# A hybrid decoder trunk on one core: scaling on GpSimd, evictions after the next split, and a new order of the first loads

## The chip, the cores and the metric

The kernel runs on one core of one Trainium2 chip. The metric is the device time of one execution in microseconds; the median of three runs is taken. A core has TensorE (matmuls; PE in the profile), VectorE (DVE), ScalarE (ACT), GpSimd (POOL) and SyncE (SP, here only a queue that issues DMAs). Each engine works through its own queue in order.

## The reference, cut to what matters

One layer on 256 rows of 2048 float32 values: a norm, one wide projection, attention with three branches beside a gated convolution, an output projection, and a gated MLP with a short convolution.

```
h     = rms_norm(x, mix_norm_g)
q, kv, gate_logits, conv_in = split(h @ w_in)
gates = sigmoid(gate_logits)
attn  = gates[0]*o_cmp + gates[1]*o_sel + gates[2]*o_win    # three softmax attentions, 16 heads
conv  = silu(layer_norm(causal_conv_31(a * sigmoid(g))))    # a, g = halves of conv_in
x     = x + concat(attn, conv) @ w_out
h     = rms_norm(x, ffn_norm_g)
x     = x + (silu(gate) * a) @ w_down                       # a, gate = causal_conv_3(h @ w_up)
out   = rms_norm(x, final_norm_g)
```

## The kernel before

Every float32 matrix product is made of three matmuls on a high and a low part (`mm3`, `mm_rows`). So each weight chunk (128 x 2048 float32, 1 MB) is loaded to `wraw` (`w_dma`, on SP's queue), split by ScalarE into the high part `wh` (L109) and by VectorE or GpSimd into the low part `wl` (L114), and then used by TensorE. Three buffers of each kind stand behind this, and the split runs two chunks ahead (`LA`). For chunks `POOLED[0] <= c < POOLED[1]` the low part is GpSimd's. `w_split` puts a chunk's split into `pieces`; `w_pump` emits them, some at each `hook`, of which each chunk has four.

The chunks in order: 0 and 1 come with the columns of x in the block `head`, loaded and split in the pieces that `CUTS` names; 2 to 15 are the convolution's gate and value tiles (`gb`, `ab`, two per j); 16 to 19 the keys and values of the compressed branch; 20 to 23 the keys; 24 to 29 the values and gates (`v_evac`); 30 to 37 the queries; then the output projection, w_up and w_down. The norm of x is not applied to x: TensorE works on x, and the evictions multiply by the inverse norm, which `x_rstd` makes from the rows of x (`xr`), `x_diag` and `x_spread` spread into `rB`.

The order in each queue is the order in which the program emits the work. An eviction is emitted after its chunk's last matmul, ahead of the next chunk's `w_next`. Lists of small steps are emitted at the hooks: `steps`, and `side`, the 30 taps of the long convolution on VectorE (L363), whose pace a planner's clock sets (`fill`). `tab_neg` (L283) and, seven hooks later, `tab_rel` (a matmul, L287) make the table of position biases.

During the q chunks from the second on, `attn_tick` advances the attention of 32 units by one stage: scores, minimum with bias (L632), exponential with its sum (L643), reciprocal (L651), scaling by reciprocal and gate (`st_scale`, L658), transposes (L664), their eviction `es` (L669) and the products (L677). The scaling of a unit is one tick ahead of its transposes. Between them run the splits, the q evictions, and the convolution's norm (`ck` is one of its small copies).

The functions that the diff touches, and their callers:

Of the kernel before, what the change touches and what calls it, by code (L numbers as in the profile page):

```python
# [18 lines left out]
T = 256  # L19
# [16 lines left out]
POOLED = (3, 30)  # L36

CUTS = ((0, 2), (2, 4), (4, 8), (8, 12), (12, 16))
# [8 lines left out]
def hybrid_trunk(ctx: ExitStack, tc: tile.TileContext, a: dict, out: bass.AP):  # L47
# [32 lines left out]
    raws, parts, pieces = {}, {}, []  # L80
    clock = {"pe": 0.0, "dve": 0.0}
# [43 lines left out]
    def w_next(cuts=1, ahead=LA):  # L125
        c = st["use"]
        st["use"] += 1
        w_pump()
        while st["split"] <= min(c + ahead, len(chunks) - 1):
            w_pump()  # L130
            w_split(cuts)
        if cuts == 1:
            w_pump()
        return parts.pop(c)
# [54 lines left out]
    with ExitStack() as mx:  # L189
# [9 lines left out]
        def load_small():  # L199
            nc.scalar.dma_start(oh, a["onehot"])  # L200
            nc.scalar.dma_start(rbn[:32], a["rel_slots"])
            nc.scalar.dma_start(cw, a["conv_vecs"])
# [7 lines left out]
        for n, (lo, hi) in enumerate(CUTS):  # L210
            w = 512 * (hi - lo)
            tile_, c0 = (ha, at) if n < 3 else (hb4[n - 3], 0)
# [4 lines left out]
        w_dma()  # L217
# [3 lines left out]
        w_dma()  # L221
        w_dma()
# [162 lines left out]
        for j in range(8):  # L385
            gb, ab = [b[:, :T] for b in bank[2 * (j if j < 3 else (j + 1) % 2):][:2]]
            if j == 0:
# [6 lines left out]
                w_pump()  # L394
                x_rstd()
# [4 lines left out]
                load_small()  # L400
                first = gb, ab
                continue
            tile_chunk(gb)
            if j == 1:
                steps[:0] = [x_diag, lambda: None, x_spread]
                tile_chunk(ab)
                glu(0, first[1], glu_gate(first[0]))
                glu(1, ab, glu_gate(gb))
            else:
                sg = glu_gate(gb)  # L410
                tile_chunk(ab)
                glu(j, ab, sg)
# [70 lines left out]
        for n in range(4):  # L483
            tile_chunk(bank[n][:, :T])
# [4 lines left out]
            for r in range(2):  # L489
# [4 lines left out]
                nc.scalar.activation(k_l[o, r, q, br], k_l[h, r, q, br].bitcast(F32), AF.Copy)  # L494

# [24 lines left out]
        for t in range(2):  # L520
            v_evac(t, 0, vb[t][:, :256])
# [13 lines left out]
        for t in range(2):  # L535
            v_evac(t, 1, vb[t][:, :256])
            gsrc = vb[t][:, 256:304].rearrange("p (q r g b) -> p b q g r", q=2, r=2, g=4)
            for br in range(3):
                nc.scalar.activation(gates[:, br, :, t].rearrange("p (q g r) -> p q g r", q=2, r=2),
                                     gsrc[:, br], AF.Sigmoid, scale=rc[:, t:t + 1])  # L540

        nc.vector.tensor_scalar(alive, wb[:, 0, CU0:CU0 + 1], BIG / 2, None, op0=OP.is_lt)
# [549 lines left out]
```

## Time and profile before

| | before |
|---|---|
| median of 3 runs | 1164.25 us (1162.98 to 1164.31) |
| the profiled execution, its own time | 1164.46 us |
| its span, first to last instruction | 1162.7 us |
| mean granted TensorE clock | 0.993 |
| TensorE busy | 1136.0 us |
| VectorE, ScalarE, GpSimd busy | 748.7, 582.3, 128.2 us |

Times in the rows are in us from the span's start unless marked ns. A granted clock of 1.00 is full speed. A wait is put down to the instruction that ended it. The prediction takes its terms from one execution and sums them against that execution's own time.

### The profile page before, as it was taken

How to read it: one execution, taken by the hardware profiler on the slowest of the kernel's cores; microseconds unless marked ns; L12 is line 12 of the kernel's file. 1: busy time of each engine (PE TensorE's matmuls, PEld its weight loads, DVE VectorE, ACT ScalarE, POOL GpSimd, SP SyncE). 2: the span in 40 equal slices, each digit the busy share in tenths (PEclk: the TensorE clock that was granted, in tenths of full speed). 3: DMA queues.
4: the chain of work that ended last, by engine and by line, in shares of the span. 5: the costliest groups of instructions: out<-in, count | busy, mean ns of one | idle time of the engine just before them, and what ended most of it. 6: DMA issues, size and time to landing. Idle time of an engine off the chain costs nothing.

```text
span 1162.7 us, 18834 instructions
## 1 busy us (share of the span) xinstructions
PE 1136.0 (98%) x7890; PEld 1058.0 (91%) x7890; DVE 748.7 (64%) x1162; ACT 582.3 (50%) x810; POOL 128.2 (11%) x80
## 2 busy tenths in 40 slices
PE   8999999889899999999999999999999999999997
PEld 8999999888778899999999999999999888888886
DVE  6699569676455666667666666666666655556544
ACT  6534256788754544444535444544454444444443
POOL 1979553000000000000000000000000000000000
PEclk9999999999999999999999999999999999999998
DMA  9567416222264545545554545454545555555551
GB/s 367 194 240 260 152 53 252 73 79 94 70 265 152 211 169 194 204 160 183 181 215 147 198 174 209 145 215 171 196 149 210 191 182 203 185 185 181 182 180 73
DMA packets 32290, 207.62 MB, mean 179 GB/s; under 512 B 3867, under 2 KB 6187, under 8 KB 8012
## 3 DMA queue, kind: packets, MB, share of 16 engines
q1 hardware_dynamic: 28592, 199.64, 48.0%
q10 hardware_dynamic: 3612, 6.76, 1.6%
q8 instruction: 62, 1.02, 0.4%
q14 instruction: 24, 0.20, 0.1%
HBM read 204.27 MB, written 2.12 MB: 178 GB/s over the span
## 4 chain that ended last, share of the span: by engine, by line
PE 87%; ACT 5%; DVE 4%; DMA 2%; issue 1%; POOL 1%; DVEq 0%; POOLq 0%; ACTq 0%
PE bank L139 18%; PE bank L137 18%; PE bank L138 18%; PE bank L146 9%; PE bank L145 9%; PE bank L144 9%; DMA xr<-in_x 2%; ACT wh L109 1%; PE bank L437 1%; ACT e L643 1%; DVE wl L114 1%; PE bank L677 1%; ACT e L658 1%; PE bank L664 1%; POOL wl L114 0%
## 5 line engine op out<-in xcount | busy, mean ns | idle before, releaser
L137 PE MATMUL bank<-xt_h,wh 128*128 128x256 f32 x1920 | 546.9, 285 | 1.8 <-ACT wh L238 1.7
L139 PE MATMUL bank<-xt_h,wl 128*128 128x256 f32 x1920 | 544.8, 284 | 1.8 <-POOL wl L114 1.5
L138 PE MATMUL bank<-xt_l,wh 128*128 128x256 f32 x1920 | 544.5, 284 | 0.0
L114 DVE TENSOR_TENSOR wl<-wraw,wh 128x2048 fp32r<-128x2048 f32 (+1 forms) x185 | 360.6, 1967 | 126.9 <-ACT wh L109 126.8
L109 ACT ACTIVATE wh<-wraw 128x2048 fp32r<-128x2048 f32 (+2 forms) x239 | 352.7, 1501 | 135.7 <-PE bank L146 68.7
L137 PEld LDWEIGHTS bank<-xt_h,wh 128*128 128x128 f32 x1920 | 369.3, 192 | 3.9 <-ACT wh L238 2.5
L139 PEld LDWEIGHTS bank<-xt_h,wl 128*128 128x128 f32 x1920 | 369.3, 192 | 2.4 <-POOL wl L114 1.7
L138 PEld LDWEIGHTS bank<-xt_l,wh 128*128 128x128 f32 x1920 | 369.5, 192 | 0.7
L900 ACT ACTIVATE yt<-u,vecs 128x256 f32<-128x256 f32 x88 | 53.0, 603 | 204.0 <-DVE u L898 204.0
L144 PE MATMUL bank<-wh,gh 128*128 128x512 f32 (+1 forms) x360 | 140.8, 391 | 0.0
L146 PE MATMUL bank<-wh,gl 128*128 128x512 f32 (+1 forms) x360 | 140.8, 391 | 0.0
L145 PE MATMUL bank<-wl,gh 128*128 128x512 f32 (+1 forms) x360 | 140.8, 391 | 0.0
L903 DVE SCALAR_TENSOR_TENSOR yt<-u,vecs,yt 128x255 f32<-128x255 f32 (+1 forms) x176 | 85.1, 484 | 62.2 <-ACT yt L900 59.1
L114 POOL TENSOR_TENSOR wl<-wraw,wh 128x1024 fp32r<-128x1024 f32 (+1 forms) x54 | 120.7, 2271 | 36.1 <-ACT wh L109 36.1
L173 POOL TENSOR_TENSOR rstd<-ms,half 128x1 f32<-128x1 f32 x4 | 2.2, 549 | 876.0 <-DVE ms L166 876.0
L363 DVE SCALAR_TENSOR_TENSOR bank<-us,cw,bank 128x256 f32<-128x256 f32 x232 | 93.7, 483 | 4.2 <-ACT bank L358 3.7
L146 PEld LDWEIGHTS bank<-wh,gl 128*128 128x128 f32 x360 | 67.8, 188 | 15.8
L145 PEld LDWEIGHTS bank<-wl,gh 128*128 128x128 f32 x360 | 67.8, 188 | 15.8
L144 PEld LDWEIGHTS bank<-wh,gh 128*128 128x128 f32 x360 | 67.8, 188 | 15.8
L892 ACT ACTIVATE gh<-gt 128x1024 fp32r<-128x1024 f32 x22 | 23.3, 1059 | 64.6 <-PE bank L145 64.6
L898 DVE TENSOR_TENSOR u<-bank,rB 128x256 f32<-128x256 f32 x88 | 37.0, 420 | 26.3 <-PE bank L139 26.3
L893 DVE TENSOR_TENSOR gl<-gt,gh 128x1024 fp32r<-128x1024 f32 x22 | 27.0, 1225 | 41.0 <-ACT gh L892 41.0
(179 smaller groups left out, 860.4 us busy)
## 6 DMA issues: line engine op xcount, KB each, us to landing
wraw<-in_w_u SPq DMA_DIRECT2D x88, 1024.0 KB, 5.0
wraw<-in_w_d SPq DMA_DIRECT2D x44, 1024.0 KB, 4.9
wraw<-in_w_t SPq DMA_DIRECT2D x30, 1024.0 KB, 4.8
wraw<-in_w_o SPq DMA_DIRECT2D x16, 1024.0 KB, 4.9
wraw<-in_w_vg SPq DMA_DIRECT2D x4, 608.0 KB, 3.7
hb<-in_head SPq DMA_DIRECT2D x2, 1024.0 KB, 10.8
xr<-in_x SPq DMA_DIRECT2D x2, 1024.0 KB, 16.9
wb<-rel_scratch ACTq DMA_DIRECT2D x1, 2048.0 KB, 10.8
```

The lines of the kernel that those rows point to most:

```text
L109: nc.scalar.activation(h[:, sl], raw[:, sl], AF.Copy)
L114: (nc.gpsimd if pooled else nc.vector).tensor_sub(l[:, sl], raw[:, sl], h[:, sl].bitcast(F32))
L137: nc.tensor.matmul(ps, wh, xh, start=first, stop=False)
L138: nc.tensor.matmul(ps, wh, xl, start=False, stop=False)
L139: nc.tensor.matmul(ps, wl, xh, start=False, stop=last)
L144: nc.tensor.matmul(ps, xh, wh, start=first, stop=False)
L145: nc.tensor.matmul(ps, xh, wl, start=False, stop=False)
L146: nc.tensor.matmul(ps, xl, wh, start=False, stop=last)
L363: nc.vector.scalar_tensor_tensor(y[:, j] if last else acc[0], us[:, j, k:k + T], cw[:, j, k:k + 1], acc[0], op0=OP.mult, op1=OP.add)
L898: nc.vector.tensor_mul(u, bank[:, :T], rB)
L900: nc.scalar.activation(yt, u, AF.Identity, scale=fcw[:, c, 2:3], bias=fcw[:, c, 3:4])
L903: nc.vector.scalar_tensor_tensor(yt[:, d:], u[:, :T - d], fcw[:, c, k:k + 1], yt[:, d:], op0=OP.mult, op1=OP.add)
```

## The change

In words, part by part:

- `st_scale`: the two multiplications of a unit go from ScalarE to GpSimd.
- `POOLED` is (5, 32) in place of (3, 30): chunks 3 and 4 get their low part from VectorE, chunks 30 and 31 from GpSimd.
- A list `late`: evictions are put on it, and `w_next` of the next chunk emits them after that chunk's call of the split; for a pooled chunk the whole split is emitted first. This holds for the convolution's gates and values from j = 2 on, the keys, the values and gates, and the queries.
- `CUTS` has six pieces in place of five: k-tiles 4 to 8 come in two loads of 512 KB.
- The loads of chunks 2, 3 and 4 are issued in front of the rows of x; before, only chunk 2 was. The three small loads go from ScalarE's queue to SP's, behind x.
- `x_rstd` and two memsets move behind the first tile of j = 1, and the spread and the first two convolution tiles' evictions become steps of the chunk after j = 1.

```diff
-POOLED = (3, 30)
-
-CUTS = ((0, 2), (2, 4), (4, 8), (8, 12), (12, 16))
+POOLED = (5, 32)
+
+CUTS = ((0, 2), (2, 4), (4, 6), (6, 8), (8, 12), (12, 16))
...
+    late = []
...
         while st["split"] <= min(c + ahead, len(chunks) - 1):
             w_pump()
             w_split(cuts)
-        if cuts == 1:
+        if cuts == 1 or POOLED[0] <= st["split"] - 1 < POOLED[1]:
             w_pump()
+        now = late[:]
+        late.clear()
+        for f in now:
+            f()
         return parts.pop(c)
...
         def load_small():
-            nc.scalar.dma_start(oh, a["onehot"])
-            nc.scalar.dma_start(rbn[:32], a["rel_slots"])
-            nc.scalar.dma_start(cw, a["conv_vecs"])
+            nc.sync.dma_start(oh, a["onehot"])
+            nc.sync.dma_start(rbn[:32], a["rel_slots"])
+            nc.sync.dma_start(cw, a["conv_vecs"])
...
-            tile_, c0 = (ha, at) if n < 3 else (hb4[n - 3], 0)
+            tile_, c0 = (ha, at) if n < 4 else (hb4[n - 4], 0)
...
-        w_dma()
+        for _ in range(3):
+            w_dma()
         xr = [ap.tile([P, D], F32, name=f"xr{t}", tag=tg) for t, tg in enumerate(("y", "us"))]
         for t in range(2):
             nc.sync.dma_start(xr[t], x_rows[:, t])
-        w_dma()
-        w_dma()
+        load_small()
...
                 w_pump()
+                first = gb, ab
+                continue
+            tile_chunk(gb)
+            if j == 1:
                 x_rstd()
                 tok = ap.tile([P, 2, 5, P], F32, name="tok", tag="tok")
                 nc.gpsimd.memset(tok[:, :, 4], 0.0)
                 us = ap.tile([P, 8, PADT], F32, name="us", tag="us")
                 nc.gpsimd.memset(us[:, :, :TAPS - 1], 0.0)
-                load_small()
-                first = gb, ab
-                continue
-            tile_chunk(gb)
-            if j == 1:
-                steps[:0] = [x_diag, lambda: None, x_spread]
                 tile_chunk(ab)
-                glu(0, first[1], glu_gate(first[0]))
-                glu(1, ab, glu_gate(gb))
+                steps[:0] = [x_diag, x_spread, lambda: glu(0, first[1], glu_gate(first[0])),
+                             lambda gb=gb, ab=ab: glu(1, ab, glu_gate(gb))]
             else:
-                sg = glu_gate(gb)
+                sg = []
+                late.append(lambda gb=gb, sg=sg: sg.append(glu_gate(gb)))
                 tile_chunk(ab)
-                glu(j, ab, sg)
+                late.append(lambda j=j, ab=ab, sg=sg: glu(j, ab, sg[0]))
...
+        for n in range(4):
+            tile_chunk(bank[n][:, :T])
+            late.append(lambda n=n: k_evac(n))
...
-        for t in range(2):
-            v_evac(t, 0, vb[t][:, :256])
+        late.extend(lambda t=t, src=vb[t][:, :256]: v_evac(t, 0, src) for t in range(2))
...
+        late.append(vg_evac)
...
-                nc.scalar.activation(e[:, lo:hi], e[:, lo:hi], AF.Copy, scale=lsum[:, br, t:t + 1])
+                nc.gpsimd.tensor_scalar_mul(e[:, lo:hi], e[:, lo:hi], lsum[:, br, t:t + 1])
...
+        def q_out(i):
+            q_evac(i, bank[i % 2])
+            if i % 2:
+                cbst["q"] = i // 2 + 1
+                cmp_branch(i // 2)
...
             tile_chunk(bank[i % 2][:, :T], TICKS[min(i, 2)])
-            q_evac(i, bank[i % 2])
-            if i % 2:
-                cbst["q"] = i // 2 + 1
-                cmp_branch(i // 2)
+            late.append(lambda i=i: q_out(i))
```

`k_evac(n)` holds the lines that stood in the loop over the keys (L485 to L494), and `vg_evac` those of the second values and the gates (L535 to L543), unchanged.

## Rows read from the trace of the kernel before

**Rows 1.** Page, busy us of each engine, share of the span, instructions.

```profile
PE 1136.0 (98%) x7890; PEld 1058.0 (91%) x7890; DVE 748.7 (64%) x1162; ACT 582.3 (50%) x810; POOL 128.2 (11%) x80
```

**Rows 2.** Windows: length, busy us by engine as headed, clock, DMA share, GB/s.

```profile
core 0: us, PE busy (x) PEld busy (x) DVE busy (x) ACT busy (x) POOL busy (x), PEclk, DMA share, GB/s
...
200.00:320.00 120.00, 108.78 (x729) 98.53 (x728) 76.89 (x252) 97.93 (x281) 1.41 (x5) 0.99 0.25 85
320.00:1140.00 820.00, 819.59 (x5579) 758.41 (x5578) 508.39 (x532) 381.75 (x363) 1.10 (x2) 1.00 0.52 185
```

**Rows 3.** TensorE's waits, 0 to 40 us: us in total, times, longest.

```profile
PE bank L137 <- ACT wh L238: 1.7, 2, 1.5
PE bank L139 <- POOL wl L114: 1.5, 1, 1.5
```

**Rows 4.** Windows of 3.4 us, columns as in rows 2.

```profile
9.80:13.20 3.40, 1.66 (x12) 1.27 (x11) 3.37 (x8) 3.38 (x8) 0.00 (x0) 1.00 1.01 424
13.20:16.60 3.40, 3.40 (x19) 3.40 (x18) 3.40 (x8) 3.40 (x9) 0.00 (x0) 0.50 1.03 434
...
170.20:173.60 3.40, 3.40 (x18) 3.40 (x18) 2.07 (x6) 2.38 (x7) 2.49 (x2) 0.50 0.08 17
...
221.40:224.80 3.40, 3.40 (x18) 3.40 (x17) 0.00 (x0) 2.05 (x7) 0.00 (x0) 0.50 0.00 0
```

**Rows 5.** Timeline of TensorE: start, us, line, what, [idle before <- releaser].

```profile
169.94 0.39 PE L517 MATMUL bank<-wl,xt_h 128*128 128x256 f32 x1 [1.99 <-POOL wl L114]
...
173.82 0.28 PE L518 MATMUL bank<-wh,xt_l 128*128 128x256 f32 x1
173.94 0.28 PE L516 MATMUL bank<-wh,xt_h 128*128 128x256 f32 x1
```

**Rows 6.** Timeline of all engines, 162 to 168 us.

```profile
162.68 0.43 DVE L487 TENSOR_TENSOR bank<-bank,rB 128x256 f32<-128x256 f32 x1
...
163.14 0.38 ACT L491 ACTIVATE k_h<-bank 64x256 fp32r<-64x256 f32 x1 [3.19 <-DVE bank L487]
...
166.40 2.00 ACT L109 ACTIVATE wh<-wraw 128x1024 fp32r<-128x1024 f32 x2
167.54 4.68 POOL L114 TENSOR_TENSOR wl<-wraw,wh 128x1024 fp32r<-128x1024 f32 x2 [4.66 <-ACT wh L109]
```

**Rows 7.** TensorE's waits, 200 to 320 us.

```profile
PE bank L677 <- ACT es L669: 3.4, 5, 1.4
PE bank L664 <- ACT ck L741: 3.2, 2, 1.9
PE bank L681 <- ACT pct L598: 1.2, 1, 1.2
```

**Rows 8.** Waits of the whole span, two of VectorE's.

```profile
DVE ma_l L684 <- ACT ma_h L683: 22.0, 8, 6.1
...
DVE bank L487 <- PE bank L139: 9.6, 1, 9.6
```

**Rows 9.** Groups of ScalarE, 200 to 320 us: count, busy us, mean ns, idle before.

```profile
L658 ACT ACTIVATE e<-e,lsum 128x256 f32<-128x256 f32 x32 | 15.9, 497 | 0.0
...
L658 ACT ACTIVATE e<-e,lsum 128x128 f32<-128x128 f32 x32 | 12.6, 394 | 2.5 <-DVE lsum L652 2.3
```

**Rows 10.** Timeline of ScalarE in the head.

```profile
9.22 1.71 ACT L233 ACTIVATE xt_h<-ha 128x256 fp32r<-128x256 f32 x4 [0.99 <-DMA ha<-in_head]
...
16.24 1.14 ACT L238 ACTIVATE wh<-hb 128x512 fp32r<-128x512 f32 x2
```

**Rows 11.** Chain that ended last, 0 to 30 us: start, us, what.

```profile
4.81 18.23 DMA xr<-in_x
```

**Rows 12.** Timeline of GpSimd, 24 to 66 us.

```profile
27.44 37.77 POOL L114 TENSOR_TENSOR wl<-wraw,wh 128x1024 fp32r<-128x1024 f32 x16
```

**Rows 13.** Groups of VectorE, 200 to 320 us.

```profile
L114 DVE TENSOR_TENSOR wl<-wraw,wh 128x1024 fp32r<-128x1024 f32 x20 | 24.3, 1221 | 1.3 <-ACT wh L109 1.2
```

**Rows 14.** Groups of GpSimd, whole span.

```profile
masks.py:199 POOL TENSOR_SCALAR_AFFINE_SELECT ident<-ident 128x128 f32<-128x128 f32 x1 | 0.3, 293 | 0.1
```

**Rows 15.** Timeline of VectorE, 55 to 66 us.

```profile
55.96 9.28 DVE L283 TENSOR_SCALAR rbn<-rbn 32x16 f32<-32x16 f32 x1
```

More of the change, by code (lines that the diff above doesn't have):

```diff
@@ L482, in hybrid_trunk, with k_evac @@
         k_l = ap.tile([P, 2, 2, 2, T], F32R, name="k_l", tag="kT")
-        for n in range(4):
-            tile_chunk(bank[n][:, :T])
+        def k_evac(n):
             br, q = divmod(n, 2)
@@ L534, in hybrid_trunk, with vg_evac @@
                     clock["pe"] += 0.35
[L535 to L542, printed above, removed]
-        nc.vector.tensor_scalar_mul(gates[:, 0, :, 0], gates[:, 0, :, 0], alive)
+        def vg_evac(vb=vb):
+            for t in range(2):
+                v_evac(t, 1, vb[t][:, :256])
+                gsrc = vb[t][:, 256:304].rearrange("p (q r g b) -> p b q g r", q=2, r=2, g=4)
+                for br in range(3):
+                    nc.scalar.activation(gates[:, br, :, t].rearrange("p (q g r) -> p q g r", q=2, r=2),
+                                         gsrc[:, br], AF.Sigmoid, scale=rc[:, t:t + 1])
+            nc.vector.tensor_scalar(alive, wb[:, 0, CU0:CU0 + 1], BIG / 2, None, op0=OP.is_lt)
+            nc.vector.tensor_scalar_mul(gates[:, 0, :, 0], gates[:, 0, :, 0], alive)
+        late.append(vg_evac)
         qs = ap.tile([P, 4, 2, T], F32R, name="qs", tag="w1")
```

## The prediction, made before the changed kernel was run

> **What bounds the kernel now.** First the page's busy times [rows 1]: TensorE is busy 1136.0 of 1162.7 us. An edit can therefore only win what TensorE loses, and the question is where it loses. The busy times by stretch answer it [rows 2]: from 320 to 1140 us it is busy without a break (819.59 of 820.00), while from 200 to 320 us, where the attention runs between the q chunks, it is busy for 108.78 of 120.00. The losses are there, in the head (0 to 40) and around 170 us. The last 8 us, after the last matmul, are not touched.
>
> In the head, TensorE's waits [rows 3] are 1.7 us for ScalarE's split of the head (L238) and 1.5 us for GpSimd's subtraction of chunk 3 (L114). The short stretches [rows 4] add what a wait can cost beyond itself: in 9.8 to 13.2 TensorE was busy 1.66 of 3.40 us at clock 1.00, and in the next 3.4 us the granted clock was 0.50, the 1.2 GHz level. The same 0.50 stands at 170.2 and at 221.4, each behind a wait. At half speed 3.4 us do 1.7 us of work: each costs 1.7 us.
>
> At 169.94 the second v chunk waits 1.99 us for GpSimd [rows 5]. The timeline before it [rows 6] shows why: the k eviction's multiply came at 162.68, ScalarE stood 3.19 us until it, then made the eviction's copies, and only at 166.40 the split of that v chunk; GpSimd followed from 167.54 with 4.68 us. The split is queued behind an eviction.
>
> In the attention, TensorE's waits [rows 7] name ScalarE: 3.4 us for `es`, 3.2 for `ck`, 1.2 for `pct`. ScalarE is busy 97.93 of 120.00 us [rows 2], and VectorE in turn waits 22.0 us for ScalarE at `ma_l` alone [rows 8]. ScalarE is the co-bottleneck; its scalings (L658) are 32 of 497 ns and 32 of 394 ns [rows 9], 28.5 us of that stretch.
>
> **Head: six cuts, three chunks in front of x.** A matmul of 256 columns follows the next after 0.12 us (173.82, 173.94) [rows 5], so a chunk of 48 takes 5.76 us and the head's 96 take 11.5. The third cut now waits 0.99 us for its 1024 KB and then 1.71 us for four activations before a weight is split [rows 10]. Cut in two, the first half has half the bytes and half the activations, so the 1.5 us wait shrinks to a few tenths, and with it, I take, the half clock behind it. The whole 3.4 us is not won, since ScalarE's own queue then sets the pace: its last cut starts weights at 16.24 [rows 10], and even if that moves up little, TensorE ends its last 24 matmuls at about 16.9 + 2.9 + 0.2 = 20.0. Before, 5.9 + 11.5 + waits of about 2.5 + 1.7 put that end near 22. Gain 2.0 us; bounds 0 (half clock comes anyway) and 2.3.
>
> Chunk 3's 1.5 us wait [rows 3]: the DMA of x took until 23.04 (4.81 + 18.23) [rows 11] and chunk 3 stood behind it, and so did GpSimd's queue with the pow of x's norm. Now two 1 MB chunks go ahead (about 2.5 us each at 434 GB/s [rows 4]) and chunks 3 and 4 are subtracted by VectorE, which idles then. Gain 1.5 us. x lands about 5 us later, near 28.5. Behind it are VectorE's sums of squares, pow, two memsets, and GpSimd's first pooled chunk, now chunk 5. Before, GpSimd's run began at 27.44 [rows 12], 4.4 us after x; so now at about 33. Chunk 5 is due at 20.0 + 3 x 5.76 = 37.3, its first half ready at 35.4: covered by 1.9 us. If that cover goes (x later than 30.5), each further us is one of TensorE's. The norm's spread, now in chunk 4 at about 33.7, needs the pow at about 32.5: covered by a us. The small loads move from ScalarE's to SP's queue in front of chunk 5; they are a fifth of a chunk and cost nothing under the same cover. **Head: 3.5 us.**
>
> **Evictions behind the split.** With a pooled chunk the split is now issued whole at the chunk's start and the eviction after it. Three or so us of eviction leave ScalarE's queue ahead of the v chunk's split, which then runs at the end of the preceding TensorE chunk rather than at 166.40; it needs to come 1.99 us earlier. Gain 1.99 and the half clock at 170.2 [rows 4], together 3.7 us; bounds 0 and 3.7. The added wait: VectorE's k_l subtraction and what is queued behind it (conv taps) now wait for up to 2.00 us of split on ScalarE [rows 6], four times. VectorE has that room, since it stands 9.6 us for TensorE at the first k eviction [rows 8]. Chunks 30 and 31 leave VectorE (four halves of 1.22 us [rows 13], 4.9 us) just before the first scores, which offsets TensorE's earlier arrival. From chunk 32 on nothing is pooled, and there the order of evictions and splits hardly changes. **Middle: 3.7 us.**
>
> **The scaling on GpSimd.** It takes 28.5 us off ScalarE, 0.8 us per unit after overlap at its edges. GpSimd's price is not shown. From below, a one-input operation of 128 columns takes 293 ns [rows 14]; from above, 16 two-input ones of 1024 columns take 37.77 us [rows 12], 2.3 ns a column. Bounds for the pair (384 columns): 0.6 us (two operations at 293 ns) and 0.9 (384 x 2.3 ns). I take 0.8: the columns of the second piece are twice the first's, so two at 293 ns are too few, and with one tensor input it is under the upper bound. It is due one tick later (120 us for some 37 ticks, 3.2 us), so either is hidden, but where the reciprocal comes late it ends 0.1 to 0.3 us later than ScalarE's: 0.5 us in all. Of the 11.2 us lost, a direct count (0.8 us off each wait of [rows 7] whose queue held one scaling pair and did not itself wait for VectorE) gives 4; if VectorE's 22.0 us waits for ScalarE shrink as well, the 7.8 us of those three rows could go. Between them I take 6, nearer the direct count, plus 1.7 for the half clock at 221.4. **Attention: 7.7 - 0.5 = 7.2 us** (bounds 1, as in A below, and 9.5).
>
> **Sum.** 3.5 + 3.7 + 7.2 = 14.4 us from the profiled execution's 1164.46, which is 0.2 above the median: 1150.0. Nothing later is touched, and TensorE is solid there, so an early gain carries to the end.
>
> **Rivals.** *A: VectorE holds the attention.* Several waits (the 1.2 for `pct`, `es` behind a late q eviction) end where ScalarE itself stood for VectorE; taking the scaling away then brings 1 us and the half clock stays. For: VectorE is busy 76.89 of 120 [rows 2] with 2 us reductions in its queue. Against: it waits longest for ScalarE [rows 8]. Time: 1164.5 - 3.5 - 3.7 - 1 = 1156.3.
>
> *B: GpSimd's long runs hold up VectorE.* At 55.96 a 32x16 VectorE operation (L283) took 9.28 us and ended at 65.24 [rows 15], just when GpSimd's 16 unbroken subtractions ended (27.44 + 37.77 = 65.21) [rows 12]. That run now begins at about 33 and may go one chunk longer, to 66, since ScalarE's split no longer stands behind the gate's sigmoid; TensorE asks for L283's result at the rel-table matmul, near 64. Price: 2 us and a half clock of 1.7. It happens only if GpSimd has not run dry at about 61.5, and by my starts that is a matter of half a us. The gate mask (L543) behind chunk 31's subtraction could add 1 to 2. Time 1150 + 4 = 1154, with both 1156. The Trainium skill (GPSIMD Engine Reference, 8. Key points) says that GpSimd shares its SBUF interfaces with VectorE, with contention where VectorE runs a 2-port mode or has two SBUF inputs; L283's 9.28 us agree with the first; no row shows the second. By the page's second case, a pair that meets one of VectorE's 20 subtractions there (24.3 of 120 us [rows 13], so one pair in five) would wait some 1.2 us more; 6 such are 8 us over two engines with cover, an estimate of 0 to 4 us at TensorE, 1150 to 1154.
>
> *C: slower.* The scaling pair comes onto TensorE's path in each of 32 ticks: transposes wait for it. The tick gives it about 3 us, so a pair of 0.8 has 2 us of cover; from 3.2 us on each pair costs its excess, and with 7.2 us of gains elsewhere it decides from an excess of 7.2 / 32 = 0.23 us. At 3.7 us a pair: 1164.5 - 7.2 + 32 x 0.5 = 1173. Only mutual blocking with VectorE could do it.
>
> *D: the orders change and the waits don't* (x later, the split still late because VectorE is): only the attention gains, 1157.
>
> **Chances.** Forecast (1146 to 1153) 0.54; A 0.15; B 0.16; D 0.07; C 0.05, and 0.03 for a sum of small losses that leaves no change. The range 1146 to 1158 holds the first four but for about 0.12 that all ScalarE waits go or that A and B meet. About 0.2% (2.3 us) is what a measurement of this kernel can tell from no change. Faster 0.92 (0.54 + 0.15 + 0.16 + 0.07), same 0.03, slower 0.05.
>
> **What would show it.** Right: TensorE's waits in the head hold no L139 for GpSimd, the granted clock is 1.00 at 13, 170 and 221 us, no wait at L517, TensorE over 114 of 120 us in the attention with ScalarE near 72, and GpSimd there 25 to 35 us. Wrong: a wait at L287's matmul near 64 us (B), VectorE's waits for ScalarE gone and TensorE still idle 9 us (A), TensorE waiting for GpSimd at the transposes (C).

## The result and the profile after

The changed kernel takes 1153.97 us (median of 4 runs, 1153.86 to 1155.27) against 1164.28 us (4 runs, 1162.98 to 1165.78) for the kernel before on the same chip: a ratio of 0.9914, with a 95% interval of 0.9896 to 0.9931. That is faster by 10.3 us, where the sum in the prediction gave 14.4. The time lies inside the range of 1146 to 1158, above the forecast's own range of 1146 to 1153. The prediction had also put rival B's first price at 1154 and rival A at 1156.3, so the time alone does not say which mechanism was right; the stages and the experiments have to.

Where the 10.3 us came from is read off by where TensorE stands in each trace. The points are first matmuls of a stage, in us from the start of the span:

| TensorE begins | before | after | gained in the stage up to here | forecast |
|---|---|---|---|---|
| chunk 2, the first behind the head's two | 22.20 | 20.78 | 1.42 | 2.0 |
| chunk 5 | 41.69 | 38.50 | 1.77 | 1.5 |
| the second column half of v (L531, now L537) | 177.17 | 170.28 | 3.70 | 3.7 |
| third q chunk, from which every hook has attention work | 202.76 | 195.87 | 0.00 | 0 |
| second chunk of the output projection, attention done | 316.96 | 306.32 | 3.75 | 7.2 |
| end of the span | 1162.66 | 1152.19 | -0.17 | 0 |

First the page's busy times after:

```profile
PE 1130.9 (98%) x7890; PEld 1053.1 (91%) x7890; DVE 742.7 (64%) x1164; ACT 563.0 (49%) x748; POOL 186.1 (16%) x144
```

Then windows of the changed kernel (columns as in rows 2): the head, the attention, and the places of the three half clocks of [rows 4]:

```profile
0.00:40.00 40.00, 36.85 (x277) 35.71 (x278) 25.30 (x53) 27.62 (x48) 9.54 (x14) 1.00 0.84 331
...
200.00:320.00 120.00, 110.85 (x720) 98.50 (x719) 72.56 (x235) 79.85 (x215) 58.90 (x70) 1.00 0.27 98
...
13.20:16.60 3.40, 1.94 (x14) 1.74 (x15) 3.37 (x8) 3.40 (x9) 0.00 (x0) 1.00 1.00 424
170.20:173.60 3.40, 3.40 (x27) 3.40 (x26) 3.40 (x10) 2.15 (x4) 3.40 (x4) 1.00 0.25 39
221.40:224.80 3.40, 2.78 (x18) 2.20 (x18) 2.89 (x9) 3.35 (x9) 3.39 (x4) 1.00 0.28 43
```

TensorE is busy 5.1 us less than in [rows 1] for the same 7890 matmuls: the three stretches at clock 0.50 [rows 4] are gone, and each had cost some 1.7 us of busy time. The rest of the gain was idle time. Busy time is not the kernel's time, though. Three executions of the kernel before show a mean clock of 0.999, where the profiled one shows 0.993. That leaves room for one such stretch at most, and they took 1162.69 to 1162.87 us, only 1.6 to 1.8 us less than 1164.46. So losing at least two of the three stretches was worth less than 2 us there, and not 2 x 1.7; one reason is given under Head below. In 200 to 320 us TensorE is busy for 110.85 us, up from 108.78 [rows 2] and not over 114 as the forecast needed. GpSimd's 58.90 us there are some twice the 25 to 35 that were forecast. ScalarE is at 79.85 us, where near 72 was forecast. This window now holds 13.7 us behind the attention; in the attention's own stretch, tabled below, ScalarE has 74.0 us and TensorE 9.2 us of idle time.

TensorE's waits after, 0 to 40 us (us in total, times, longest):

```profile
PE bank L142 <- ACT wh L243: 1.9, 2, 1.4
...
PE bank L144 <- DVE wl L244: 0.2, 1, 0.2
```

And for 200 to 320 us:

```profile
PE bank L672 <- POOL e L666: 6.9, 9, 1.4
PE bank L685 <- ACT es L677: 1.5, 3, 0.6
PE bank L149 <- DVE mn L640: 0.4, 1, 0.4
PE bank L689 <- ACT pct L606: 0.2, 1, 0.2
```

In the head the wait for GpSimd [rows 3] is gone, and the one for ScalarE is not: 1.9 us in place of 1.7. In the attention the 7.8 us for ScalarE in [rows 7] have become 1.7 us (`es`, `pct`), the wait for `ck` is gone, and a new one of 6.9 us stands in their place: the transposes (L672) wait for the scaled exponentials `e` from GpSimd. (`mn` is the minimum that VectorE takes for a unit, `pct` the transposed weights of the compressed branch.) These are GpSimd's scalings in that stretch, grouped by line and shape (busy us, mean ns, idle before):

```profile
L666 POOL TENSOR_SCALAR e<-e,lsum 128x256 f32<-128x256 f32 x32 | 37.8, 1180 | 0.0
L666 POOL TENSOR_SCALAR e<-e,lsum 128x128 f32<-128x128 f32 x32 | 20.9, 652 | 54.7 <-DVE lsum L660 42.1 <-PE bank L144 12.5
```

And the longest waits of the other engines there:

```profile
POOL e L666 <- DVE lsum L660: 42.1, 13, 11.9
DVE ma_l L692 <- ACT ma_h L691: 19.9, 8, 6.6
```

A pair takes 1.83 us where 0.8 was forecast, between bounds of 0.6 and 0.9. GpSimd is no bottleneck by load: it runs two pairs at a time, and ahead of 13 of its 16 such runs it stands idle until VectorE has the reciprocal sums (L660). VectorE's own wait at `ma_l` (the low part of an attention output), 22.0 us before [rows 8], is 19.9 us, hardly less, although ScalarE has been relieved.

### The profile page after: what moved, and what is told of

Read it like the earlier page. It is cut to its first block, busy times and chain, and to the rows that moved or that the text cites. A ratio compares the mean times of both kernels' runs of the same rounds, so it can differ in the third digit from the quotient of the medians.

```text
span 1152.2 us, 18870 instructions
## 1 busy us (share of the span) xinstructions
PE 1130.9 (98%) x7890; PEld 1053.1 (91%) x7890; DVE 742.7 (64%) x1164; ACT 563.0 (49%) x748; POOL 186.1 (16%) x144
## 4 chain that ended last, share of the span: by engine, by line
PE 89%; DVE 4%; ACT 3%; issue 2%; DMA 1%; POOL 1%; SPq 0%; POOLq 0%; DVEq 0%; ACTq 0%
PE bank L142 19%; PE bank L144 19%; PE bank L143 19%; PE bank L151 9%; PE bank L150 9%; PE bank L149 9%; DVE wl L115 1%; DMA hb<-in_head 1%; POOL e L666 1%; PE bank L685 1%; ACT wh L110 1%; PE bank L672 1%; DVE e L640 0%; ACT e L651 0%; PE bank L539 0%
## 5 line engine op out<-in xcount | busy, mean ns | idle before, releaser
L666 POOL TENSOR_SCALAR e<-e,lsum 128x128 f32<-128x128 f32 x64 | 57.7, 916 | 54.7 <-DVE lsum L660 42.1
```

What stands on the lines that cost most here:

```text
L666: nc.gpsimd.tensor_scalar_mul(e[:, lo:hi], e[:, lo:hi], lsum[:, br, t:t + 1])
```

## The experiments

Twelve kernels ran, each beside the kernel before on the same chip. For the attention all are compared on one stretch, from TensorE's first matmul of the third q chunk to its first of the second output chunk, with the same 692 matmuls inside (686 in tick_more, where the order differs). The table is from windows of exactly that stretch, with TensorE's idle time as its length less its busy time. The ends of matmuls are modelled, so idle sums carry about 1 us; the lengths don't.

| kernel | length, us | TensorE idle | VectorE busy | ScalarE busy | GpSimd busy | clock | median, us |
|---|---|---|---|---|---|---|---|
| before | 114.20 | 11.2 | 71.3 | 93.2 | 1.4 | 0.99 | 1164.3 |
| changed | 110.45 | 9.2 | 71.4 | 74.0 | 58.9 | 1.00 | 1154.0 |
| scale_back | 112.65 | 11.2 | 71.3 | 93.1 | 1.4 | 1.00 | 1158.5 |
| quarter_scale | 109.40 | 8.6 | 71.2 | 74.0 | 36.0 | 1.00 | 1153.0 |
| psum_low | 110.29 | 8.1 | 71.6 | 74.5 | 53.8 | 1.00 | 1154.2 |
| piece_each | 110.46 | 9.6 | 71.3 | 84.8 | 28.6 | 1.00 | 1154.4 |
| branch_each | 111.45 | 10.2 | 71.2 | 83.9 | 33.6 | 1.00 | 1156.6 |
| scale_vec | 117.30 | 14.3 | 85.9 | 74.3 | 1.4 | 0.99 | 1162.2 |
| tick_more | 117.59 | 13.7 | 72.7 | 74.1 | 59.8 | 0.96 | 1161.5 |
| pool_q_low | 134.18 | 23.5 | 75.0 | 94.1 | 22.7 | 0.91 | 1179.1 |

**scale_back: the scaling back on ScalarE, the rest of the change kept.**

```diff
-                nc.gpsimd.tensor_scalar_mul(e[:, lo:hi], e[:, lo:hi], lsum[:, br, t:t + 1])
+                nc.scalar.activation(e[:, lo:hi], e[:, lo:hi], AF.Copy, scale=lsum[:, br, t:t + 1])
```

> The changed kernel with the 64 scalings of the attention back on ScalarE, all else as changed. Theory 1 (GpSimd's pair of 1.5 to 2.6 us lies on TensorE's path and eats half of what ScalarE wins): the attention from the first q chunk to the first chunk of the output projection's second group loses what the move had won there, 3.75 us, and the time is 1154.0 + 3.75 = 1157.7; TensorE idles about 11 us there, none of it for GpSimd. Rival A (VectorE's order holds the attention, whoever scales): the time stays within 1 us of 1154.

Measured: 1158.48 us (1156.11 to 1160.93), ratio to before 0.9953 (0.9937 to 0.9968); the profiled execution took 1157.71 us, theory 1's 1157.7, though by other parts. TensorE's waits in the attention are those of before to a tenth:

```profile
PE bank L685 <- ACT es L677: 3.4, 5, 1.4
PE bank L672 <- ACT ck L749: 3.2, 2, 1.9
PE bank L689 <- ACT pct L606: 1.2, 1, 1.2
```

Yet the stretch is 1.55 us shorter than before, because no half clock stands behind these same waits. So of the 3.75 us gained in the attention only 2.20 are the scaling's by these traces, and the half clock at 221.4 us can go without it. ScalarE's relief is 93.1 - 74.0 = 19.1 us, 0.6 us a unit and not 0.8: successive activations overlap in the records by more than I took off. The other 1.5 us by which this profiled execution is behind the changed kernel lie in the head, where it has a half clock (window 16.00 to 19.40 us at 0.50) behind the same 1.4 us wait. One trace does not settle the half clocks: three of this kernel's six executions show mean clocks of 0.994 or 0.995 and took 1159.25 to 1160.93 us, while the changed kernel's four show 0.996 to 0.998. The medians lie 4.5 us apart. Whether the scaling on GpSimd makes half clocks rarer stays open.

**quarter_scale: GpSimd scales a quarter of each piece's columns.** The other three quarters stay unscaled.

```diff
-                nc.gpsimd.tensor_scalar_mul(e[:, lo:hi], e[:, lo:hi], lsum[:, br, t:t + 1])
+                q = lo + (hi - lo) // 4
+                nc.gpsimd.tensor_scalar_mul(e[:, lo:q], e[:, lo:q], lsum[:, br, t:t + 1])
```

> The changed kernel, but GpSimd scales only the first quarter of each piece's columns (three quarters of the scalings are left out). Theory 1 (what limits the gain in the attention is the length of GpSimd's scaling: 0.65 + 1.18 us a pair, and TensorE's transposes wait 6.9 us for it there): a piece of 32 or 64 columns takes 0.3 to 0.5 us, TensorE's wait for GpSimd at the transposes falls from 6.9 us to under 2, the idle time in 200 to 320 us falls from 9.1 to 4 or 5, and the time is 1149 to 1150 (ratio to before 0.987 to 0.988). Rival A (VectorE's order of work sets the end; the transposes' wait for GpSimd only shows where it ends): other waits take its place and the time stays within 1 us of the changed kernel's 1154.

Measured: 1152.98 us (1152.80 to 1154.19), ratio 0.9899 (0.9884 to 0.9914); the attention's stretch is 1.05 us shorter. Its scalings, grouped, 200 to 320 us:

```profile
L667 POOL TENSOR_SCALAR e<-e,lsum 128x64 f32<-128x64 f32 x32 | 23.6, 737 | 0.0
L667 POOL TENSOR_SCALAR e<-e,lsum 128x32 f32<-128x32 f32 x32 | 12.5, 390 | 75.1 <-DVE lsum L660 57.9 <-PE bank L144 17.1
```

TensorE's waits, 190 to 312 us:

```profile
PE bank L673 <- POOL e L667: 3.0, 4, 1.1
PE bank L673 <- ACT ck L750: 2.5, 2, 1.4
PE bank L686 <- ACT es L678: 2.1, 4, 0.8
```

The wait for GpSimd falls by 3.9 us and TensorE gets 1.05 of it: `ck` ends late instead, `es` takes 2.1 us in place of 1.5 and `mn` 0.8 in place of 0.4. Shortening a pair from 1.83 to 1.13 us is worth 1 us and not 4 or 5; theory 1 fell, the rival was right to a microsecond.

**psum_low: nothing for GpSimd to share with VectorE.** VectorE's subtraction takes its second operand from PSUM for chunks 32 to 38, so those low parts are w less zero.

```diff
+            if 32 <= c < 39:
+                v = lambda x: x[:, sl].rearrange("p (a c) -> p a c", c=P)
+                nc.vector.tensor_sub(v(l), v(raw), bank[3][:, None, 384:].to_broadcast([P, n // cuts // P, P]))
+            else:
+                (nc.gpsimd if pooled else nc.vector).tensor_sub(l[:, sl], raw[:, sl], h[:, sl].bitcast(F32))
...
+        nc.vector.memset(bank[3][:, 384:], 0.0)
```

> The changed kernel, but VectorE's subtraction of the weights' low parts for chunks 32 to 38 takes its second operand from a PSUM bank (zeros, repeated) and not from the high part in SBUF, so those low parts are not the reference's; size and number of the operations stay. Theory 1 (GpSimd's scaling stands still while VectorE runs an operation with two SBUF inputs: 1.71 us beside 0.92 us of the subtraction, 0.92 alone): all 256-column scalings that met a subtraction fall from 1.71 to about 0.95 us, GpSimd's 58.9 us in 200 to 320 fall to about 50, TensorE's wait for GpSimd at the transposes falls from 6.9 to 3 or 4 us, and the time by 1 to 3 us, to 1151 to 1153. Rival (the long ones are long for another reason, for instance where they lie in the tick): they stay at 1.71 us and the time at 1154.

Measured: 1154.24 us (1154.11 to 1155.48), ratio 0.9915 (0.9901 to 0.9928). GpSimd's timeline in the changed kernel (first fence) and here (second); each row is two pairs back to back:

```profile
207.25 4.05 POOL L666 TENSOR_SCALAR e<-e,lsum 128x128 f32<-128x128 f32 x4 [4.24 <-DVE lsum L660]
213.33 2.98 POOL L666 TENSOR_SCALAR e<-e,lsum 128x128 f32<-128x128 f32 x4 [2.03 <-DVE lsum L660]
...
276.19 4.02 POOL L666 TENSOR_SCALAR e<-e,lsum 128x128 f32<-128x128 f32 x4 [2.64 <-DVE lsum L660]
```

```profile
207.99 3.00 POOL L671 TENSOR_SCALAR e<-e,lsum 128x128 f32<-128x128 f32 x4 [4.18 <-DVE lsum L665]
214.12 2.99 POOL L671 TENSOR_SCALAR e<-e,lsum 128x128 f32<-128x128 f32 x4 [3.13 <-DVE lsum L665]
...
276.28 4.03 POOL L671 TENSOR_SCALAR e<-e,lsum 128x128 f32<-128x128 f32 x4 [2.45 <-DVE lsum L665]
```

TensorE's waits in this kernel, 190 to 312 us:

```profile
PE bank L677 <- POOL e L671: 3.6, 6, 1.2
PE bank L690 <- ACT es L682: 1.8, 3, 0.8
PE bank L677 <- ACT ck L754: 1.4, 1, 1.4
```

The mechanism is shown: the burst at 207 us takes 3.00 us once the subtraction beside it has only one operand in SBUF, and the burst at 276 us, beside a subtraction of a later chunk that was left as it was, still takes 4.03. Of the changed kernel's ten 256-column scalings of over 1.7 us five are left: four beside subtractions of later chunks, which are as before, and one beside another VectorE operation. The expected price is not there: TensorE's wait for GpSimd falls from 6.9 to 3.6 us, `ck` takes 1.4 of it, and the stretch is 0.16 us shorter. Theory 1 was right on the durations and wrong on the time.

**piece_each and branch_each: the scaling shared between GpSimd and ScalarE.** The one gives ScalarE the 256-column piece of every unit, the other all of the first branch's units.

```diff
+                if t == 0:        # branch_each: if br:
                     nc.gpsimd.tensor_scalar_mul(e[:, lo:hi], e[:, lo:hi], lsum[:, br, t:t + 1])
+                else:
+                    nc.scalar.activation(e[:, lo:hi], e[:, lo:hi], AF.Copy, scale=lsum[:, br, t:t + 1])
```

> The changed kernel, but only the 128-column piece of a unit is scaled by GpSimd and the 256-column piece by ScalarE (0.5 us each), so that the two run side by side. Theory 1 (the pair of 1.5 to 2.6 us on GpSimd is what TensorE's transposes wait for, and ScalarE had 40 us to spare after the change): waits for GpSimd nearly gone, ScalarE some 96 of 120 us, 1151 to 1154. Rival (ScalarE's queue is late by order and not by load, so that any scaling in it brings its waits for es and ck back): 1155 to 1158, as with one branch on each engine (1156.6).

> The changed kernel, but the units of the first branch are scaled by ScalarE again and only those of the second by GpSimd. Theory 1 (a pair on GpSimd is too long where its reciprocal comes late, one on ScalarE costs 0.9 us of a full queue): GpSimd's waits halve, ScalarE's come back by half, and the time lies between that of the changed kernel and that of the one with all scalings on ScalarE (1154.0 and 1158.5) or below both, 1152 to 1156. Rival (the waits are set by contention of GpSimd with VectorE and not by the length of GpSimd's queue): the units that stay on GpSimd wait as long each as before, and the time is halfway, 1156.

Measured: piece_each 1154.38 us (1154.05 to 1155.92), ratio 0.9918 (0.9905 to 0.9930), its stretch as long as the changed kernel's to 0.01 us. TensorE's wait for GpSimd is down to 1.7 us there, and ScalarE's are back (`es` 2.5, `ck` 1.7). So GpSimd's load could be halved without a gain and ScalarE's raised by 10.8 us without a loss. branch_each: 1156.56 us (1156.32 to 1158.29), ratio 0.9932 (0.9920 to 0.9945); 1.0 us of its distance is in the attention, 1.4 us are a half clock in the head of its profiled execution. Neither beats the changed kernel.

**scale_vec: the scaling on VectorE.**

```diff
-                nc.gpsimd.tensor_scalar_mul(e[:, lo:hi], e[:, lo:hi], lsum[:, br, t:t + 1])
+                nc.vector.tensor_scalar_mul(e[:, lo:hi], e[:, lo:hi], lsum[:, br, t:t + 1])
```

> The changed kernel with the scaling on VectorE in place of GpSimd. A 128-column operation of this kind took VectorE 0.29 us in the head; I take 0.75 us a pair, 24 us, VectorE then busy 97 of 120 us in 200 to 320. Theory 1 (GpSimd's length and its standstill beside VectorE's subtractions hold TensorE): with a pair half as long and nothing to contend with, TensorE's wait for the scaling goes from 6.9 to under 3 us, 1150 to 1153. Rival A (VectorE's order of work holds the attention, so that more work in its queue costs TensorE directly): waits for VectorE's results (mn, pcb, e) take their place, 1156 to 1165.

Measured: 1162.19 us (1160.92 to 1162.44), ratio 0.9981 (0.9972 to 0.9991). VectorE's scalings (ns: least, median, most):

```profile
L666 DVE TENSOR_SCALAR e<-e,lsum x64: 279/316/351, 200.4 to 305.6; 128x128 f32<-128x128 f32 x32, 128x256 f32<-128x256 f32 x32
```

The longest waits of TensorE there, 190 to 312 us:

```profile
PE bank L685 <- ACT es L677: 3.9, 4, 1.6
PE bank L672 <- ACT ck L749: 3.2, 2, 2.2
PE bank L672 <- DVE e L666: 1.5, 2, 1.0
```

A pair takes VectorE 0.6 us, a third of GpSimd's 1.83, and TensorE's wait for the scaling itself does fall to 1.5 us. But 14.4 us more work on VectorE make the stretch 6.85 us longer, of which one half clock (257 us) is about 1.7. ScalarE has the same 74 us of work as in the changed kernel, and TensorE waits for it again, 7.1 us in these two rows: ScalarE is late because what it needs from VectorE is. From 196 to 313 us its waits for VectorE's `mn` and `q` are 13.3 us, and 8.1 in the changed kernel. Rival A was right here: work put on VectorE comes out at TensorE, about a third of it even without the half clock ((6.85 - 1.7) / 14.4).

**pool_q_low: the converse, VectorE relieved.** The scaling is on ScalarE and GpSimd takes the subtractions up to chunk 37.

```diff
-POOLED = (5, 32)
+POOLED = (5, 38)
```

> The changed kernel with the scalings back on ScalarE and GpSimd taking the subtractions of the weights' low parts of the first q chunks too (chunks 5 to 37 in place of 5 to 31). This frees VectorE in the attention of about 2.4 us per q chunk. Theory 1 (ScalarE is the co-bottleneck of the attention there; VectorE waits for it): VectorE's relief does not shorten TensorE's waits for ScalarE, and a subtraction of 4.7 us on GpSimd is later than one of 2.4 on VectorE: the time is that of the kernel with the scalings on ScalarE, 1158.5, or up to 3 us longer. Rival A (VectorE's order of work holds the attention): it falls by 2 to 4 us, to 1154 to 1156.

Measured: 1179.06 us (1176.96 to 1180.52), ratio 1.0122 (1.0108 to 1.0137). That is far above what either theory expected, and inconclusive: the subtractions now share GpSimd's queue with the memsets of `ec`, one of which waits 25.5 us for VectorE's `pcb`, and TensorE's longest new wait is 7.1 us for `pcb` (L604). The order broke before the relief of VectorE could show.

**tick_more: one tick more between scaling and transposes** (a fifth buffer with it).

```diff
-        D_S, D_T = 3, 4
+        D_S, D_T = 3, 5
```

> The changed kernel with one more tick between a unit's scaling and its transposes (D_T 5 in place of 4, one more buffer of e). Theory 1: TensorE's 6.9 us of waits for GpSimd at the transposes go, the scaling off ScalarE then brings what was forecast for it, and the time is about 1154.0 - 5 = 1149. Rival A: the transposes were late because VectorE's reciprocal, minimum and copies are late; the waits move to other lines and the time stays within 1 us of 1154.

Measured: 1161.46 us (1157.90 to 1166.14), ratio 0.9979 (0.9964 to 0.9995): a miss. The waits for GpSimd fall to 3.9 us, but everything behind the transposes lands in other ticks: `es` 2.9 us, L725 for `es` 1.8, `q` 1.4, `mn` 1.1, and the clock of the stretch is 0.96. The half clocks are not all of the loss: two executions with a mean clock of 0.998, as high as the changed kernel's, took 1157.90 and 1158.08 us. The distances between the steps are part of the order.

**late_only: the late evictions alone, on the kernel before.** The pooled split is issued whole at the chunk's start, and evictions follow it; nothing else is changed.

```diff
-        if cuts == 1:
+        if cuts == 1 or POOLED[0] <= st["split"] - 1 < POOLED[1]:
             w_pump()
+        now = late[:]
+        late.clear()
+        for f in now:
+            f()
...
-        for n in range(4):
-            tile_chunk(bank[n][:, :T])
+        def k_evac(n):
...
+            late.append(lambda n=n: k_evac(n))
```

> The kernel before with one part of the change alone: evictions queued behind the next chunk's split, and the pooled split issued whole. Theory 1 (the step on the middle): the wait of 1.99 us at the second v chunk and the half clock behind it go, and nothing else does: 1164.3 - 3.7 = 1160.6 (ratio 0.9968). Rival (the late evictions pay in the compressed branch in front of v, as the kernel without them showed, and the wait at the v chunk goes only with the other parts): TensorE still waits 1 to 2 us at the second v chunk, and the time is within 1 us of 1164.3.

Measured: 1162.56 us (1160.62 to 1165.70), ratio 0.9982 (0.9971 to 0.9993). TensorE begins v's second column half at 173.48 us: 3.69 us earlier than before, with nothing else changed up to there. The window that had the half clock:

```profile
170.20:173.60 3.40, 3.40 (x30) 3.40 (x29) 3.37 (x10) 2.11 (x4) 1.55 (x2) 1.00 0.31 127
```

The step stands by itself, and four of the ten executions took 1160.62 to 1161.13 us, where 1160.6 was expected; the median is 2 us above that. In the profiled one part of the gain is given back at once, by the largest of TensorE's waits from 140 to 200 us:

```profile
PE bank L144 <- DVE wl L115: 1.0, 1, 1.0
```

At 188.27 us TensorE waits for VectorE's low part of an early q chunk. In the changed kernel GpSimd makes that part (chunks up to 31), and the wait is not there. By these two traces the shift of `POOLED` covers the late evictions' own cost. The rest of this execution's loss, 2.0 us, lies in the attention (116.16 us), where it has two half clocks and the kernel before one.

**no_late: evictions at once, on the changed kernel.** `late` runs what it is given immediately; the pooled split is still issued whole.

```diff
-    late = []
+    class Now(list):
+        def append(self, f):
+            f()
...
+    late = Now()
```

> The changed kernel with every eviction emitted right after its chunk again, ahead of the next chunk's split. Theory 1 (the split queued behind the k eviction was the cause at the second v chunk): the wait of about 2 us at that chunk and the half clock behind it return, 1154.0 + 3.7 = 1157.7. Rival: chunks 3, 4, 30 and 31 in other hands or the shifted steps had removed it, then no wait returns and the time stays at 1154.

Measured: 1160.83 us (1159.60 to 1161.99), ratio 0.9973 (0.9962 to 0.9984). TensorE's waits, 140 to 200 us:

```profile
PE bank L472 <- DVE hd L465: 2.2, 1, 2.2
PE bank L476 <- DVE hd L465: 1.2, 1, 1.2
```

The first ends at 151.88 us and the second at 153.47. The two windows from there on:

```profile
152.70:156.10 3.40, 2.63 (x25) 2.49 (x26) 2.62 (x7) 0.62 (x2) 0.00 (x0) 0.50 0.40 156
156.10:159.50 3.40, 3.40 (x21) 3.40 (x20) 2.34 (x7) 2.85 (x7) 0.00 (x0) 0.60 0.00 0
```

The wait at the v chunk did not come back; a worse one came in the compressed branch, 3.4 us of waits and 6.8 us at clock 0.50 (151.96 to 158.79 us). There `hd` (the branch's hidden values, on VectorE) stands behind GpSimd's memset and ScalarE's sigmoid. This does not show that the split issued whole is enough for the v chunk: TensorE comes to the v chunks 6.8 us later than in the changed kernel (165.58 against 158.76 us), which gives GpSimd that much more time. What it shows is that the late evictions are needed in the compressed branch. The kernel without them is not the order of before.

**five_cuts: the head in five cuts again.**

```diff
-CUTS = ((0, 2), (2, 4), (4, 6), (6, 8), (8, 12), (12, 16))
+CUTS = ((0, 2), (2, 4), (4, 8), (8, 12), (12, 16))
```

> The changed kernel with the head in five pieces again, the three chunks still in front of x. Theory 1 (the smaller third piece shortens the wait and with it keeps the clock): the wait of 1.5 us in front of the third piece and the half clock return, the first chunk after the head starts 1.4 us later than in the changed kernel, and the time is 1155.4. Rival: the head is ScalarE's in any case and the start of that chunk stays within 0.3 us, 1154.

Measured: 1154.34 us (1154.09 to 1155.82), ratio 0.9919 (0.9906 to 0.9931). Chunk 2 begins at 20.76 us with five cuts and at 20.78 with six. TensorE's longest wait in 0 to 40 us:

```profile
PE bank L142 <- ACT wh L243: 2.3, 2, 1.6
```

The window of that wait and the one behind it:

```profile
9.20:12.60 3.40, 1.60 (x11) 1.19 (x10) 2.77 (x6) 3.34 (x8) 0.00 (x0) 1.00 0.98 414
12.60:16.00 3.40, 3.40 (x31) 3.40 (x30) 3.40 (x9) 3.40 (x9) 0.00 (x0) 1.00 1.01 426
```

The wait is as long as before [rows 3], and no half clock follows it here. With six cuts the same wait has moved one cut back: ScalarE's conversions of x for the fifth cut begin at 12.15 us, 0.88 us late for its 1 MB, and TensorE waits 1.41 us until 14.44. The cuts bring nothing that can be measured.

**x_first: the rows of x loaded ahead of chunks 3 and 4 again.**

```diff
-        for _ in range(3):
-            w_dma()
+        w_dma()
         xr = [ap.tile([P, D], F32, name=f"xr{t}", tag=tg) for t, tg in enumerate(("y", "us"))]
...
+        w_dma()
+        w_dma()
         load_small()
```

> The changed kernel with one part undone: the rows of x are loaded ahead of the weight chunks 3 and 4 again. Theory 1 (the step on chunk 3): chunk 3 lands some 5 us later, ScalarE splits it from about 26.2 us, TensorE reaches it at 26.5 and waits 1.5 to 2 us for its high and low part, though VectorE and not GpSimd subtracts it; 1155.5 to 1156 (1157.5 if a half clock follows). Rival (what made the wait was the queue of GpSimd behind the norm of x, and not the place of the load): no wait over 0.3 us at chunk 3, and 1154 as the changed kernel.

Measured: 1155.87 us (1155.54 to 1156.62), ratio 0.9929 (0.9915 to 0.9942). The window in which the head lost time:

```profile
16.00:19.40 3.40, 3.40 (x19) 3.40 (x19) 3.37 (x7) 3.40 (x6) 0.00 (x0) 0.55 1.02 429
```

The timeline of VectorE, with the low parts of chunk 3:

```profile
26.70 2.36 DVE L115 TENSOR_TENSOR wl<-wraw,wh 128x1024 fp32r<-128x1024 f32 x2 [5.76 <-ACT wh L110]
```

All 1.54 us of this execution's loss are that half clock, and TensorE waits nowhere between 20 and 60 us. It reaches chunk 3 late, at 28.08 us. At the changed kernel's 26.54 it would have asked at 26.8 for a low part that is ready at 27.9, so the order of the loads is worth some 1.1 us of the 1.77 by these rows, and the rest is GpSimd's 2.4 us a half [rows 12] against VectorE's 1.2. That split is worked out and not measured. One of the five executions had a mean clock of 0.998, where the traces with a half clock in the head show 0.997 at most, and still took 1155.87 us, 1.9 us more than the changed kernel. So the order of the loads seems to cost something without a half clock too; where, that execution does not show.

## Why the prediction was right, and where its sizes were off

**Head, 3.5 us forecast, 3.19 measured.** The sum came out nearly right, but its two terms do not add as they were told. In the kernel before, the chain that ends last in the head goes from the DMA of x [rows 11] over the norm to GpSimd's low part of chunk 3, and TensorE's third matmul of that chunk starts when it is done (from `--critical`, start and length):

```profile
27.48 2.35 POOL wl L114
29.87 0.38 PE bank L139
```

What TensorE wins ahead of 29.87 us is lost there in a longer wait. late_only, which has the head of before, shows it in small: it began chunk 2 at 22.10 us, 0.10 us sooner, waited 1.6 us for GpSimd in place of 1.5, and began chunk 5 at 41.70 us, where the kernel before did at 41.69. By these rows six cuts alone would have won nothing, and not 2.0 us; that kernel was not run. The 3.19 us came by removing this chain (no wait for GpSimd is left at chunk 3), and some 1.3 to 1.5 of them hang on there being no half clock in the head: the kernels with the chain removed and a half clock begin chunk 5 at 39.79 to 40.04 us, the changed one at 38.50.

The term for six cuts was wrong as a mechanism. "The 1.5 us wait shrinks to a few tenths" did not happen; the wait moved from the third cut to the fifth. What was measured in that row is the half clock, which the changed kernel's profiled execution does not have and the one of before has. It is not bound to the number of cuts: five_cuts had none, and before and late_only, also with five, had one, while six cuts had one in the profiled executions of scale_back, quarter_scale, branch_each, pool_q_low, no_late and x_first and none in those of the changed kernel, psum_low, piece_each, tick_more and scale_vec. With it chunk 2 begins at 22.06 to 22.32 us, without it at 20.69 to 20.90: some 1.4 us. How often it comes in each kernel stays open.

The covers held. GpSimd's first pooled chunk started at 32.67 us (33 forecast), and nothing in 20 to 140 us made TensorE wait.

**Middle, 3.7 forecast, 3.70 measured,** and 3.69 with that part alone. This is how the split got ahead of the eviction (ScalarE's timeline of the changed kernel, beside [rows 6]):

```profile
162.98 1.30 ACT L110 ACTIVATE wh<-wraw 128x608 fp32r<-128x608 f32 x2
164.71 0.38 ACT L494 ACTIVATE k_h<-bank 64x256 fp32r<-64x256 f32 x1 [0.44 <-DVE bank L490]
```

In [rows 6] the k eviction stood in front of a split at 166.40; here a split of the v weights is at 162.98, GpSimd follows from 163.75, and the eviction's copies come behind.

**Attention, 7.2 forecast, 3.75 measured: the mis-sized term.** Its three parts:

- The waits, "between them I take 6", came to 2.2 by scale_back. Two inputs were off. ScalarE was relieved by 19.1 us and not 28.5, since durations of successive activations overlap. And the waits that went were replaced, which the count by waits could not see: 7.8 us for ScalarE in [rows 7] became 6.9 us for GpSimd, and when those are taken away (quarter_scale, psum_low, piece_each) `ck`, `es` and `mn` come back. The stretch stays between 109.4 and 110.5 us.
- GpSimd's pair, 0.8 us forecast "under the upper bound" of 0.9, takes 0.60 + 0.92 = 1.52 us undisturbed (the burst of two pairs at 213.33 us: 2.98 us) and 1.83 in the mean. The bound was wrong because a cost per column from 1024 columns hides the fixed part of some 0.28 us, and one tensor input turned out no cheaper a column (2.5 ns) than two (2.3 ns [rows 12]). Cutting the pair to 1.13 us brought 1.05 us at TensorE (quarter_scale), so the 0.5 taken for 0.8 us was too little.
- The half clock at 221.4 us, 1.7 forecast, did go, 1.55 us; but scale_back's profiled execution lacks it too, with the waits of before. That the scaling earned it is not shown.

**Rival A** (VectorE holds the attention; gain 1 us, 1156.3) named a limit that the runs support, and too small a gain. Its sign, VectorE's waits for ScalarE gone, did not come. VectorE's `ma_l` wait and its busy time are nearly what they were, GpSimd idles until VectorE's reciprocals, and 14.4 us of work added to VectorE cost 6.85 us (some 5.2 without the half clock), while 10.8 us added to ScalarE cost nothing. What a lighter VectorE would bring is not shown: pool_q_low, meant for that, broke another order. So that VectorE's order sets most of the remaining 9 us is supported from one side only.

**Rival B** (GpSimd holds up VectorE) cost nothing in its first form. VectorE's 32x16 operation (now L288) took 1.41 us in place of the 9.28 of [rows 15]:

```profile
55.59 1.41 DVE L288 TENSOR_SCALAR rbn<-rbn 32x16 f32<-32x16 f32 x1
```

It ended at 57.00 us, 0.02 us behind the end of the GpSimd subtraction that it began beside (56.98). In eleven of the fourteen traces it ended like that. In five_cuts it went on to the end of the third subtraction, in before and late_only to that of the fourth, the last of the run. What decides this is not shown, so the short time was luck. But no luck was needed, as five_cuts shows:

```profile
55.81 6.17 DVE L288 TENSOR_SCALAR rbn<-rbn 32x16 f32<-32x16 f32 x1
```

There TensorE's matmul on the result began at 65.22 us without a wait, and in the changed kernel at 65.24. The price of 2 us and a half clock did not hang on this operation. The gate mask cost nothing either: from 140 to 200 us TensorE waits 0.3 us in all, for `hd`. Its second form came with the roles turned round: VectorE's subtraction keeps its 1.22 us, and GpSimd waits. The rule quoted in the prediction (the Trainium skill, GPSIMD Engine Reference, 8. Key points: contention where VectorE has two SBUF inputs) agrees with psum_low. A 256-column scaling took 1.71 us beside a subtraction that overlapped it by 0.92 us, and 0.92 us alone; ten of 32 took 1.7 us or more (nine beside such a subtraction, one beside VectorE's `y` and `ck`), some 8 us on GpSimd ((1180 - 920) ns x 32). Of the 0 to 4 us put down for TensorE, psum_low, which took away five of the ten, found 0.16.

**C** came in its sign and not in its price: the transposes wait for GpSimd 9 times in 32 units, 0.8 us each, but that took the place of waits for ScalarE. **D** did not come: the orders did move the waits.

## What to carry to other kernels

A wait that ends on one engine is not a price that goes when that engine is relieved: with several in-order queues around TensorE the next-latest result takes its place, so count a relief as the distance to the second-latest one, and test it by adding work to each engine in turn. Price a short operation on an engine from rows of its own size, at two sizes, so that fixed part and rate come apart; take the relief of a queue from busy time with and without the work, and not from a sum of durations. Two losses add only if they lie on the same chain: time won ahead of a wait that another chain ends is lost in that wait. A half clock behind a wait is a matter of the execution as much as of the kernel: book it apart from the wait, and look at the clock and time of several executions before it is put down to an edit.

## What the runs showed of the hardware

GpSimd's scaling by a column, in place, takes 0.36, 0.44, 0.60 and 0.92 us for 32, 64, 128 and 256 columns: about 0.28 us and 2.5 ns a column, where nothing lengthens it. VectorE's same operation takes 0.28 to 0.35 us for 128 and 256 columns, ScalarE's 0.39 and 0.50.

While VectorE ran an operation with two operands in SBUF, GpSimd's operation stood still almost for the time of the overlap (0.92 us of overlap, 0.79 us longer), and VectorE's subtractions lost nothing (1220 ns after, 1221 before [rows 13]). With one of the operands in PSUM the lengthening was gone (psum_low). In the other case, VectorE's 32x16 one-operand operation beside GpSimd's back-to-back subtractions, it is VectorE that waited: it ended 0.02 to 0.03 us behind the end of one of them, of the first in eleven traces (0.6 to 1.4 us), of the third in one (6.17 us) and of the fourth in two (9.28 us).

The same wait of 1.4 to 1.6 us in the head was followed by a stretch of 3.4 us at clock 0.50 in some executions and at 1.00 in others.
